# Letting a planner put five kinds of two-input operations on GpSimd instead of VectorE

## The chip, the cores and the metric

The kernel runs on one core of one Trainium2 chip. A core has five engines with queues of their own: TensorE (PE, matrix products), VectorE (DVE), ScalarE (ACT), GpSimd (POOL) and SyncE (SP, which here only issues transfers). Each works through its own instructions in the order in which they were written; semaphores between the engines make an instruction wait for what it needs. The metric is device microseconds of one execution, the median of the runs.

## The reference

A decoder block with two token mixers side by side, on 2048 tokens of 1024 channels, in float32:

```python
xn = rms_norm(x, g_pre);  proj = xn @ w_in      # r_x r_z m_x m_z m_o m_i m_f gate_r gate_m
u = causal_dwconv(r_x, rg_conv_w, rg_conv_b)    # 4 taps, then the RG-LRU
r, i = sigmoid(headwise(u, rg_w_a) + b_a), sigmoid(headwise(u, rg_w_x) + b_x)
a = exp(-8 * r * softplus(-lam));  b = sqrt(1 - a*a) * (i * u)
h_r = scan over tokens: h = a*h + b;            y_r = h_r * silu(r_z)
c = silu(causal_dwconv(m_x, ...)); q, k = headwise(c, ...); v = headwise(m_x, ...)
h_m = mlstm over chunks of 128 tokens, 4 heads of 256: gates, C and n states, running maximum
h_m = layer_norm(sigmoid(m_o) * h_m) * norm_g + skip * c;   y_m = h_m * silu(m_z)
y = sigmoid(gate_r) * (y_r @ w_branch_r) + sigmoid(gate_m) * (y_m @ w_branch_m)
out = x + rms_norm(y @ w_out, g_post)
```

## The kernel before, in words

**Tiling.** The 2048 tokens are four blocks of 512, taken two at a time (a "superblock"). Activations lie channels by tokens, 128 partitions by 512 tokens, 256 KB in a tile. Each operand of a float32 product is split into a rounded part and a rest (`split` and `wsplit`: the names end in h and l, or are `whi` and `wlo`), and a product is three matrix products (`mm3`). The rounding is a copy (a CAST in the profile, on ScalarE or VectorE), the rest a subtraction on VectorE.

**Stages.** In a superblock, `phase_a` makes the input projections with Strassen's seven products (`Pair`), runs the convolutions (`conv`, whose first three columns come from five small GpSimd operations into `hc`), the RG-LRU (`Rec`) and the gates, and stores the results in HBM. `phase_b` then takes eight heads one after another (four heads of two blocks, `Head`): `q` makes the queries, `s2` scales them with `eb` and splits them, `chunk` does the four chunks, `norm` and `back` finish the head; between them stand the products with `w_branch_r` and `w_branch_m` (`br`, `bm`) and with `w_out` (`out_half`, `out_last`), which keep TensorE fed while a head's chain runs.

**Who sets the order.** Nothing of this is emitted as it is written. `Plan` records every operation with its inputs, outputs and an estimated cost, and `order()` then runs a list schedule over the five engines: at each time an engine takes the operation with the smallest priority (its place in the program, moved by `early` and `urgent`) among those that are ready in the plan. The order it finds is what is emitted, engine by engine; on the chip each engine is bound to it. A result goes to another engine 150 ns later in the plan, and to TensorE another 400 ns later (`SYNC`, `SLACK`). An operation recorded with `either` has a second engine, which takes it when it has nothing of its own that is ready and the first engine is busy:

```python
elif item[2].seq <= limit and can(item[2]) and free[item[2].eng] > t + WORTH:
    pick = heapq.heappop(spare[e])
    op = pick[2]
    op.eng, op.cost, op.call = op.alt
```

The planner's costs in ns for n elements in a partition are, for GpSimd and for a VectorE operation with two wide inputs:

```python
if eng == "gpsimd":
    return 550 + n * 0.6, 0
...
    return 80 + 1.02 * n + (100 if len(ins) > 2 else 0), 0
```

that is 857 and 602 for 512 elements. In the kernel before, `either` serves only copies and squares, between ScalarE and VectorE (line 235 of the profile is an operation that went to its second engine, line 200 every other one). GpSimd has the small operations of `conv`, copies of states, the power -0.5 of the norms (`rstd`, `r`), a mask (`AFFINE_SELECT` on `mbc`), and issues most stores.

Of the kernel before, what the change touches and what calls it, by code (L numbers as in the profile page):

```python
# [12 lines left out]
ALU = mybir.AluOpType  # L13
# [376 lines left out]
def hybrid_kernel(ctx: ExitStack, tc: tile.TileContext, x, w_ch, w_mo, w_gate, w_q, w_k, w_v, w_out,  # L390
                  vec, gpost, bif, ident_d, triu_d, eye_d, xt_d, out):
    nc = Plan(tc.nc)
# [20 lines left out]
    def t2k(s="t", dt=F32):  # L413
        return nc.tile(tp, [P, 512], dt, "t", nm(s), ring=NSLOT - SPARE)

    def psum():
        return nc.tile(pp, [P, 512], F32, "ps", nm("ps"), ring=8)
# [19 lines left out]
    def vcol(v, j):  # L437
        return vecs[:, v, j:j + 1]
# [33 lines left out]
    def copy(out, in_):  # L472
        nc.either(("scalar", "copy", dict(out=out, in_=in_)), ("vector", "tensor_copy", dict(out=out, in_=in_)))


    def token_scale(b, keep=None):
        ss = small([P, NT, 2], "ss")
        ps = psum()
        for t in range(NT):
            r0 = b * T + t * P  # L480
            for q in range(2):
                xt = t2k("xh")
                with nc.urgent(0 if b else BPRI):
                    nc.sync.dma_start(out=xt, in_=x[r0:r0 + P, q * 512:(q + 1) * 512])
                if keep is None:
                    sq = xt
                else:
                    keep.append(xt)
                    sq = t2k("sq")
                acc = ss[:, t, q:q + 1]  # L490
                nc.either(("scalar", "activation", dict(out=sq, in_=xt, func=AF.Square, scale=1.0 / 32.0,
                                                        accum_out=acc)),
                          ("vector", "scalar_tensor_tensor", dict(out=sq, in0=xt, scalar=1.0 / D, in1=xt,
                                                                  op0=ALU.mult, op1=ALU.mult, accum_out=acc)))
            rstd = rms_scale(ss[:, t, :])
            dg = small([P, P], "dg")
            nc.vector.tensor_scalar(out=dg, in0=ident, scalar1=rstd, scalar2=None, op0=ALU.mult)
            with nc.urgent(BPRI):
                mmul(ps[:, t * P:(t + 1) * P], ones, dg, start=True, stop=True)
        rb = t2k("rb")  # L500
        with nc.urgent(BPRI):
            copy(rb, ps)
        return rb
# [290 lines left out]
    class Rec:  # L794
# [12 lines left out]
        def gate(self, bi, j, u, uhl):  # L807
            ghl = self.ghl
            th = []
            for q in range(2):  # L810
                pg = psum()
                o = (j % 2) * 256 + q * P
                mm3(pg, (ghl[0][:, o:o + P], ghl[1][:, o:o + P]), uhl, True, True)
                tt = t2k("tr")
                nc.scalar.activation(out=tt, in_=pg, func=AF.Sigmoid, bias=vcol(V_BX if q else V_BA, j))
                th.append(tt)
            nc.vector.tensor_tensor(out=u, in0=th[1], in1=u, op=ALU.mult)
            self.hold[bi, j] = (u, th[0])
            if len(self.hold) == 4:
                with nc.urgent(-LPRI):  # L820
                    self.scan()

        def scan(self):
            av = {}
            for (bi, j), (u, r) in self.hold.items():
                av[bi, j] = a = t2k("a")
                nc.scalar.activation(out=a, in_=r, func=AF.Exp, scale=nsp8[:, j:j + 1])
                nc.scalar.activation(out=r, in_=r, func=AF.Tanh, scale=sp8[:, j:j + 1])
                aq = t2k("aq")
                nc.scalar.activation(out=aq, in_=a, func=AF.Square)  # L830
                nc.vector.scalar_tensor_tensor(out=r, in0=aq, scalar=1.0, in1=r, op0=ALU.add, op1=ALU.mult)
            for u, r in self.hold.values():
                nc.scalar.activation(out=r, in_=r, func=AF.Sqrt, bias=tiny_t)
            for (bi, j), (u, r) in self.hold.items():
                nc.vector.tensor_tensor(out=u, in0=r, in1=u, op=ALU.mult)
                nc.vector.tensor_tensor_scan(out=r, data0=av[bi, j], data1=u, initial=hst.part(j)[:, j:j + 1],
                                             op0=ALU.mult, op1=ALU.add)
                nc.gpsimd.tensor_copy(out=hst.part(j)[:, j:j + 1], in_=r[:, 511:512])
                self.hr[bi, j] = r
# [143 lines left out]
    class Head:  # L983
# [91 lines left out]
        def s2(self):  # L1075
            h, cs, qs, G, eb = self.h, self.cs, self.qs, self.G, self.eb
            pS = psum()
            for c in range(NT):
                s = slice(c * P, (c + 1) * P)
                for k in range(2):  # L1080
                    mmul(pS[:, s], cs[k][:, s], qs[k][:, s], start=k == 0, stop=k == 1)
            wt = G.mbc[h]
            for c in range(NT):
                s = slice(c * P, (c + 1) * P)
                nc.scalar.activation(out=wt[:, s], in_=wt[:, s], func=AF.Exp, scale=-1.0, bias=G.A[:, c, h:h + 1])
            nc.vector.tensor_tensor(out=wt, in0=wt, in1=pS, op=ALU.mult)
            self.wt = split(wt, "wt")
            for k in range(2):
                nc.vector.tensor_tensor(out=qs[k], in0=qs[k], in1=eb, op=ALU.mult)
                qs[k] = split(qs[k], "q")  # L1090
            self.dn = small([P, NT], "dn")
            self.st = small([P, NT, 6], "st")
            self.mv = small([P, NT, 2], "mv")
# [59 lines left out]
        def back(self):  # L1153
            h, th, cs = self.h, self.th, self.cs
            for m in range(2):
                j = 2 * h + m
                pn = psum()
                for c in range(NT):
                    nc.tensor.transpose(pn[:, c * P:(c + 1) * P],
                                        th[c // 2][:, (c % 2) * DH + m * P:(c % 2) * DH + (m + 1) * P], ident)  # L1160
                nc.vector.scalar_tensor_tensor(out=cs[m], in0=pn, scalar=gh[:, j:j + 1], in1=cs[m],
                                               op0=ALU.mult, op1=ALU.add)
                tz = self.zz[m]
                nc.vector.tensor_tensor(out=tz, in0=cs[m], in1=tz, op=ALU.mult)
                nc.gpsimd.dma_start(out=self.Q["ym"][self.b % 2][j], in_=tz)


# [62 lines left out]
    def phase_b(sb, Q, fts, nxt):  # L1230
# [16 lines left out]
        def bm(bi, d, hooks=None):  # L1247
            tgd = branch(BM, d, [st["ym"]], [Q["gm"][bi][d]], {"hooks": hooks})[0]
            yp = t2k("ypl")
            with early():  # L1250
                nc.sync.dma_start(out=yp, in_=Q["yp"][bi][d])
            nc.vector.tensor_tensor(out=tgd, in0=tgd, in1=yp, op=ALU.add)
            st["y"].append(split(tgd, "y"))

        for u in range(8):
# [201 lines left out]
```

## Time and profile before

| | |
|---|---|
| median of 3 runs | 1977.0 us (1976.48 to 1977.06) |
| the profiled execution | 1975.61 us, span 1973.8 us |
| PE busy | 1955.6 us, 99% |
| DVE busy | 1600.5 us, 81% |
| ACT busy | 1158.6 us, 59% |
| POOL busy | 551.0 us, 28% |
| granted TensorE clock, mean | 0.998 |

The first superblock runs to about 1000 us, the second from there on. In each, the first half is `phase_a` (until about 560 us and 1530 us), the second `phase_b`. Busy PE time counts a matrix product from its start to its end, and the products overlap, so short delays between two of them do not show as idle time. In the rows a tile's number is left out, and digits at a name's end too.

### The profile page before, as it was taken

The page shows a single profiled execution, that of the slowest core. Times are in us where ns is not written, and L with a number is a line of the kernel's source. Part 1 is how long each engine was busy: PE and PEld are TensorE (multiplying, and loading weights), DVE is VectorE, ACT ScalarE, POOL GpSimd, SP SyncE. Part 2 cuts the span into 40 slices and gives each one's busy share as a digit, 9 for nine tenths or more (in the row PEclk, how much of TensorE's full clock was granted, in tenths as well). Part 3 has the DMA queues.
Part 4 walks back from the last instruction along what each step waited for, and adds up shares of the span by engine and source line. Part 5 has one row for each costly group of instructions (what it writes and reads, how often), then busy time and mean ns, then how long its engine had stood idle before and what let it go on. Part 6 is the DMA issues. An engine that isn't in the chain of part 4 may idle for free.

```text
span 1973.8 us, 30190 instructions
## 1 busy us (share of the span) xinstructions
PE 1955.6 (99%) x10240; PEld 1679.8 (85%) x10240; DVE 1600.5 (81%) x3052; ACT 1158.6 (59%) x2108; POOL 551.0 (28%) x864
## 2 busy tenths in 40 slices
PE   8999999999999999999999999999999999999998
PEld 8888888888898888887898888888888988888886
DVE  7997787978866889989579888788787677899783
ACT  6675665758555545654356768576585554465441
POOL 2544352443411111102037344434343111110010
PEclk9999999999999999999999999999999999999999
DMA  7224233232485557577372332413326843755661
GB/s 250 97 81 160 97 139 112 91 129 85 142 300 195 191 189 239 175 244 244 102 246 70 116 119 86 145 70 129 112 86 224 289 161 134 261 182 188 207 225 48
DMA packets 160987, 313.80 MB, mean 159 GB/s; under 512 B 19744, under 2 KB 40480, under 8 KB 160832
## 3 DMA queue, kind: packets, MB, share of 16 engines
q1 hardware_dynamic: 133440, 223.53, 34.1%
q0 software_dynamic: 27104, 88.21, 11.6%
q8 instruction: 80, 1.31, 0.3%
q14 instruction: 75, 0.61, 0.1%
q10 hardware_dynamic: 288, 0.13, 0.0%
HBM read 226.82 MB, written 84.97 MB: 158 GB/s over the span
## 4 chain that ended last, share of the span: by engine, by line
PE 96%; DVE 1%; POOL 1%; DMA 1%; issue 1%; ACT 0%; SPq 0%; POOLq 0%; ACTq 0%; DVEq 0%
PE ps L200 96%; POOL hc L200 1%; DVE wlo L200 0%; DMA xh<-in_x_dram 0%; DMA dth<-th 0%; DMA gp<-in_gpost_dram 0%; DVE o L200 0%; DVE u L200 0%; DMA dym<-mz 0%; DVE th L200 0%; POOL out_dram L200 0%; POOL rstd L200 0%; POOL r L200 0%; DVE a22l L200 0%; ACT uh L200 0%
## 5 line engine op out<-in xcount | busy, mean ns | idle before, releaser
L200 ACT CAST whi<-raw 128x512 fp32r<-128x512 f32 (+1 forms) x484 | 300.2, 621 | 469.7 <-PE ps L200 367.0
L200 DVE TENSOR_TENSOR wlo<-raw,whi 128x512 fp32r<-128x512 f32 (+1 forms) x576 | 394.6, 687 | 133.2 <-ACT whi L200 121.3
L200 DVE SCALAR_TENSOR_TENSOR u<-xq,vecs,u 128x511 f32<-128x511 f32 (+2 forms) x192 | 143.1, 745 | 8.5 <-ACT u L200 7.4
L200 DVE TENSOR_TENSOR raw<-raw,raw 128x512 f32<-128x512 f32 (+1 forms) x208 | 142.5, 687 | 1.7
L200 ACT ACT_TABLE_LOAD x89 | 114.2, 1283 | 5.9 <-DVE u L200 2.0
L200 POOL TENSOR_SCALAR h<-halo,vecs 128x2 f32<-128x2 f32 (+1 forms) x128 | 108.9, 864 | 1.3
L200 PE MATMUL ps<-ymh,wlo 128*128 128x512 f32 x256 | 100.2, 392 | 0.9 <-DVE wlo L200 0.9
L200 PE MATMUL ps<-yrh,whi 128*128 128x512 f32 x256 | 100.7, 394 | 0.0
L200 PE MATMUL ps<-yml,whi 128*128 128x512 f32 x256 | 100.5, 393 | 0.0
L200 PE MATMUL ps<-yrl,whi 128*128 128x512 f32 x256 | 100.4, 392 | 0.0
L200 PE MATMUL ps<-yrh,wlo 128*128 128x512 f32 x256 | 100.1, 391 | 0.0
L200 PE MATMUL ps<-ymh,whi 128*128 128x512 f32 x256 | 97.9, 394 | 0.5 <-ACT whi L200 0.5
L200 POOL TENSOR_SCALAR hc<-halo,vecs 128x3 f32<-128x3 f32 x64 | 81.6, 1275 | 8.1 <-DVE u L200 6.0
L200 POOL TENSOR_TENSOR rstd<-rsm,eps_t 128x1 f32<-128x1 f32 x32 | 20.2, 634 | 200.8 <-DVE rsm L200 186.1
L200 PE MATMUL ps<-a11h,whi 128*128 128x512 f32 x192 | 75.5, 393 | 0.0
L200 PE MATMUL ps<-whi,yh 128*128 128x512 f32 x192 | 75.5, 393 | 0.0
L200 PE MATMUL ps<-wlo,yh 128*128 128x512 f32 x192 | 75.1, 391 | 0.0
L200 PE MATMUL ps<-whi,yl 128*128 128x512 f32 x192 | 74.9, 391 | 0.0
L200 PE MATMUL ps<-a11l,whi 128*128 128x512 f32 x192 | 74.7, 389 | 0.0
L200 PE MATMUL ps<-a11h,wlo 128*128 128x512 f32 x192 | 74.7, 389 | 0.0
L200 PE MATMUL ps<-s3h,wlo 128*128 128x512 f32 x192 | 74.7, 389 | 0.0
L200 PE MATMUL ps<-s3h,whi 128*128 128x512 f32 x192 | 74.7, 389 | 0.0
(324 smaller groups left out, 6471.4 us busy)
## 6 DMA issues: line engine op xcount, KB each, us to landing
raw<-in_w_ch_dram SPq DMA_DIRECT2D x288, 256.0 KB, 2.8
raw<-in_w_out_dram SPq DMA_DIRECT2D x64, 256.0 KB, 2.9
raw<-in_w_mo_dram SPq DMA_DIRECT2D x48, 256.0 KB, 6.2
xh<-in_x_dram SPq DMA_DIRECT2D x32, 256.0 KB, 5.2
dth<-th POOLq DMA_DIRECT2D x32, 256.0 KB, 3.4
dgr<-tg POOLq DMA_DIRECT2D x32, 256.0 KB, 2.4
dyr<-tz POOLq DMA_DIRECT2D x32, 256.0 KB, 2.5
dmx<-xq POOLq DMA_DIRECT2D x32, 256.0 KB, 2.7
```

The lines of the kernel that those rows point to most:

```text
L200: getattr(eng.real, what)(*[real(v) for v in a], **{n: real(v) for n, v in kw.items()})
```

## The change

A helper `pair_op` records a two-input operation with VectorE first and GpSimd as the second engine, and five places use it: the product of the input gate and `u` (`gate`), the product with the square root (`scan`), the queries times `eb` (`s2`), the head's output times the silu gate (`back`), and the sum of the two branches (`bm`). There are 32 operations of each of the five, 160 in all, each 128x512 float32 with both inputs and the output in SBUF.

```diff
+    def pair_op(out, a, b, op):
+        k = dict(out=out, in0=a, in1=b, op=op)
+        nc.either(("vector", "tensor_tensor", k), ("gpsimd", "tensor_tensor", k))
...
-            nc.vector.tensor_tensor(out=u, in0=th[1], in1=u, op=ALU.mult)
+            pair_op(u, th[1], u, ALU.mult)
...
-                nc.vector.tensor_tensor(out=u, in0=r, in1=u, op=ALU.mult)
+                pair_op(u, r, u, ALU.mult)
...
-                nc.vector.tensor_tensor(out=qs[k], in0=qs[k], in1=eb, op=ALU.mult)
+                pair_op(qs[k], qs[k], eb, ALU.mult)
...
-                nc.vector.tensor_tensor(out=tz, in0=cs[m], in1=tz, op=ALU.mult)
+                pair_op(tz, cs[m], tz, ALU.mult)
...
-            nc.vector.tensor_tensor(out=tgd, in0=tgd, in1=yp, op=ALU.add)
+            pair_op(tgd, tgd, yp, ALU.add)
```

In the order that the planner makes of it, 103 of the 160 stand on GpSimd: 39 of the 64 `u<-tr,u`, 19 of the 32 `q<-q,eb`, 17 of the 32 `mz<-cs,mz` and 28 of the 32 `tgl<-tgl,ypl`. The order of the other operations changes with them on every engine, and six rounding copies go to VectorE that were on ScalarE.

The first place is the second head of the second superblock (`mz_16748` is the last product of the head before it, `q_17991` and `q_18034` are this head's queries, `wtl` and `ql` are rests that its first chunk needs). On VectorE before:

```order
L200 SCALAR_TENSOR_TENSOR cs_16738<-ps_18006,gh,cs_16738 128x512
L200 TENSOR_TENSOR mz_16748<-cs_16733,mz_16748 128x512
L200 TENSOR_TENSOR mz_16754<-cs_16738,mz_16754 128x512
L200 TENSOR_TENSOR wlo_18058<-raw_17578,whi_18024 128x512
L200 SCALAR_TENSOR_TENSOR kl_18065<-ps_18022,wg_17591,kh_18043 128x256
L200 SCALAR_TENSOR_TENSOR kl_18074<-ps_18031,wg_17591,kh_18047 128x256
L200 TENSOR_TENSOR mbc_17638<-mbc_17638,ps_18039 128x512
L200 TENSOR_TENSOR q_17991<-q_17991,eb_17726 128x512
L200 SCALAR_TENSOR_TENSOR kl_18065<-ps_18022,wg_17591,kh_18043 128x256
L200 SCALAR_TENSOR_TENSOR kl_18074<-ps_18031,wg_17591,kh_18047 128x256
L200 TENSOR_TENSOR q_18034<-q_18034,eb_17726 128x512
L200 TENSOR_TENSOR wtl_18102<-mbc_17638,wth_18090 128x512
```

Now, on VectorE, from the same place on:

```order
L200 TENSOR_TENSOR mz_16754<-cs_16738,mz_16754 128x512
L200 SCALAR_TENSOR_TENSOR kl_18062<-ps_18022,wg_17591,kh_18044 128x256
L200 SCALAR_TENSOR_TENSOR kl_18070<-ps_18031,wg_17591,kh_18049 128x256
L200 TENSOR_TENSOR mxl_18075<-mxr_17891,mxh_18013 128x512
L200 SCALAR_TENSOR_TENSOR kl_18062<-ps_18022,wg_17591,kh_18044 128x256
L200 SCALAR_TENSOR_TENSOR kl_18070<-ps_18031,wg_17591,kh_18049 128x256
L200 TENSOR_TENSOR mbc_17638<-mbc_17638,ps_18040 128x512
L200 TENSOR_TENSOR cl_18096<-cs_17909,ch_18065 128x512
L200 TENSOR_TENSOR ql_18103<-q_17991,qh_18094 128x512
L200 TENSOR_TENSOR wtl_18110<-mbc_17638,wth_18100 128x512
L200 TENSOR_TENSOR ql_18116<-q_18034,qh_18106 128x512
```

And on GpSimd:

```order
L200 TENSOR_TENSOR r_4139_17958<-r_4138_17944,eps_t 128x4
L235 TENSOR_TENSOR mz_16748<-cs_16733,mz_16748 128x512
L200 DMA dym_18052<-mz_16748 128x512
L200 DMA dym_18067<-mz_16754 128x512
L235 TENSOR_TENSOR q_17991<-q_17991,eb_17726 128x512
L235 TENSOR_TENSOR q_18034<-q_18034,eb_17726 128x512
```

One of the two `mz` products and both query products went over; they stand behind one another on GpSimd, with two store issues between, and VectorE does the rests `mxl` and `cl` where the products were.

The second place is on TensorE in `phase_a`, at the fourth gate product of a projection group (`uh` and `ul` are the parts of the convolved `u`, `gwh` and `gwl` those of its weights, `s1h` and `s1l` belong to the projection that runs meanwhile). Before:

```order
L200 MATMUL ps_5023<-s1h_620,whi_4956 128x512
L200 MATMUL ps_5023<-s1l_635,whi_4956 128x512
L200 MATMUL ps_5023<-s1h_620,wlo_4969 128x512
L200 MATMUL ps_5023<-s1h_665,whi_4956 128x512
L200 MATMUL ps_5023<-s1l_678,whi_4956 128x512
L200 MATMUL ps_5023<-s1h_665,wlo_4969 128x512
L200 MATMUL ps_5023<-s1h_707,whi_4956 128x512
L200 MATMUL ps_5023<-s1l_725,whi_4956 128x512
L200 MATMUL ps_5046<-uh_5030,gwh_4315 128x512
L200 MATMUL ps_5048<-uh_5030,gwh_4315 128x512
```

Now:

```order
L200 MATMUL ps_5026<-uh_5011,gwh_4315 128x512
L200 MATMUL ps_5030<-uh_5011,gwh_4315 128x512
L200 MATMUL ps_5034<-s1h_620,whi_4956 128x512
L200 MATMUL ps_5034<-s1l_635,whi_4956 128x512
L200 MATMUL ps_5026<-ul_5022,gwh_4315 128x512
L200 MATMUL ps_5026<-uh_5011,gwl_4332 128x512
```

The gate product has moved ahead of eight products of the projection; this is so in five of the eight projection groups, and with seven products in a sixth. On VectorE the first of the products with `u` that stood in front of this gate's rest `ul` (`u_4866<-tr_4985,u_4866`) has gone to GpSimd.

The third place is TensorE in the sixth head of the first superblock (`ymh`, `yml` belong to the branch product that fills the time, `wtl` and `qh` to the head's first chunk). Between the last product `q,cs` and the first that uses `qh` stood 24 products of 128x512 and 9 of 128x258; now there are 17 and 9. The rows ahead of the first use, before and then now:

```order
L200 MATMUL ps_9149<-ymh_7862,whi_9007 128x512
L200 MATMUL ps_9149<-yml_7946,whi_9007 128x512
L200 MATMUL ps_9149<-ymh_7862,wlo_9019 128x512
L200 MATMUL ps_9149<-ymh_7889,whi_9007 128x512
L200 MATMUL ps_9149<-yml_8224,whi_9007 128x512
L200 MATMUL ps_9131<-vh_8900,wtl_9145 128x258
L200 MATMUL ps_9131<-ch_8853,qh_9084 128x258
```

```order
L200 MATMUL ps_9089<-ymh_8236,whi_8949 128x512
L200 MATMUL ps_9089<-yml_8316,whi_8949 128x512
L200 MATMUL ps_9089<-ymh_8236,wlo_8963 128x512
L200 MATMUL ps_9089<-ymh_8245,whi_8949 128x512
L200 MATMUL ps_9089<-yml_8323,whi_8949 128x512
L200 MATMUL ps_9133<-vh_8920,wtl_9135 128x258
L200 MATMUL ps_9133<-ch_8848,qh_9131 128x258
```

The first chunk's product with the queries now comes before the branch product's second half is through, where it came after the next branch product had begun.

## The prediction

> **What bounds the kernel now.** I read the page's busy line and the shares of its chain of waits first, then what TensorE waited for, then the stages.
>
> ```profile
> PE 1955.6 (99%) x10240; PEld 1679.8 (85%) x10240; DVE 1600.5 (81%) x3052; ACT 1158.6 (59%) x2108; POOL 551.0 (28%) x864
> PE 96%; DVE 1%; POOL 1%; DMA 1%; issue 1%; ACT 0%; SPq 0%; POOLq 0%; ACTq 0%; DVEq 0%
> ```
>
> ```profile
> PE ps L200 <- DMA ident<-in_ident_dram: 3.9, 1, 3.9
> PE ps L200 <- ACT uh L200: 1.6, 2, 1.1
> PE ps L200 <- DMA xh<-in_x_dram: 1.1, 1, 1.1
> PE ps L200 <- DVE wlo L200: 0.9, 2, 0.5
> PE ps L200 <- ACT a11h L200: 0.8, 1, 0.8
> PE ps L200 <- ACT rb L200: 0.7, 1, 0.7
> PE ps L200 <- ACT whi L200: 0.5, 1, 0.5
> PE ps L200 <- DVE dg L200: 0.3, 1, 0.3
> ...
> 1965.59 0.02 issue
> ```
>
> TensorE is busy for 1955.6 of 1973.8 us and holds 96% of the chain. Of the 18.2 us that it idles, the waits make 9.8 and the end 8.2 (the last row is from the chain in order of time: the last product ends at 1965.59). `ident`, `xh`, `a11h`, `rb` and the longer `uh` wait belong to the first 81 us, before the first moved operation's result could matter. What is left for any change of VectorE's load to win are the other `uh` wait (1.6 - 1.1 = 0.5), `wlo` 0.9 and `whi` 0.5: **1.9 us, 0.1% of the time**. A view by stretches shows the same, and where VectorE is dense:
>
> ```profile
> 800.00:900.00 100.00, 99.62 (x583) 87.25 (x582) 92.68 (x214) 57.08 (x128) 10.54 (x18) 1.00 0.67 227
> 1300.00:1400.00 100.00, 100.00 (x443) 82.81 (x442) 84.48 (x140) 67.49 (x102) 44.77 (x70) 1.00 0.33 113
> 1700.00:1800.00 100.00, 100.00 (x583) 87.21 (x583) 92.53 (x206) 59.83 (x134) 12.48 (x25) 1.00 0.59 198
> ```
>
> Columns: stretch, length, busy PE, PE loads, DVE, ACT, POOL. VectorE reaches 93% in `phase_b`, but TensorE is full there too. So VectorE's 81% is no bound; the question is only whether the new order makes TensorE wait.
>
> **What a moved operation costs.** VectorE's price, from its groups kept apart by shape:
>
> ```profile
> L200 DVE TENSOR_TENSOR u<-tr,u 128x512 f32<-128x512 f32 x64 | 43.8, 684 | 3.5 <-ACT tr L200 3.5
> L200 DVE TENSOR_TENSOR q<-q,eb 128x512 f32<-128x512 f32 x32 | 23.2, 740 | 1.5 <-ACT eb L200 1.0 <-PE ps L200 0.6
> L200 DVE TENSOR_TENSOR tgl<-tgl,ypl 128x512 f32<-128x512 f32 x32 | 21.8, 683 | 0.0
> L200 DVE TENSOR_TENSOR mz<-cs,mz 128x512 f32<-128x512 f32 x32 | 21.1, 682 | 0.1
> ```
>
> About 0.68 us each; two in a row take 1.29 (first row below), so one more costs 0.60. The 103 that move free 103 x 0.60 = 62 us of VectorE. No two-input 128x512 operation runs on GpSimd in this trace. The nearest is the mask, with one input of this size:
>
> ```profile
> 877.28 1.29 DVE L200 TENSOR_TENSOR q<-q,eb 128x512 f32<-128x512 f32 x2
> 617.30 1.74 DVE L200 TENSOR_TENSOR q<-q,eb 128x512 f32<-128x512 f32 x2 [0.48 <-ACT eb L200]
> 617.34 1.16 POOL L200 TENSOR_SCALAR_AFFINE_SELECT mbc<-mbc 128x512 f32<-128x512 f32 x1 [5.04 <-ACT eb L200]
> 622.35 0.63 POOL L200 TENSOR_SCALAR_AFFINE_SELECT mbc<-mbc 128x512 f32<-128x512 f32 x1 [1.67 <-ACT eb L200]
> 621.92 0.68 DVE L200 TENSOR_TENSOR mbc<-mbc,ps 128x512 f32<-128x512 f32 x1
> 468.27 0.18 POOL L200 COPY halo<-xq 128x3 f32<-128x3 f32 x1
> ```
>
> Undisturbed it takes 0.63; a copy of three elements takes 0.18, so 512 elements cost 0.45. With a second input to fetch I take 0.18 + 2 x 0.45 = **1.1 us**, an estimate; bounds 0.63 (the second input is free) and 1.27 (two masks). The planner counts on 0.86.
>
> The same rows show a second price. At 617 us the mask began beside a pair of two-input products: the pair took 1.74 instead of 1.29, and the mask 1.16 instead of 0.63. They took turns: the mask waited for the first product (0.53), the second product for the mask (0.45). At 622 us a product with one input in PSUM, `mbc<-mbc,ps`, ran beside the mask at its usual 0.68. So a two-input operation on GpSimd holds up whatever VectorE wants to do with two SBUF inputs, for up to 1.1 us, and itself waits for up to 0.68. Per moved operation VectorE gains 0.60 and loses between 0 and 1.1: between -62 us and +51 us in all. VectorE is 81% busy and roughly three quarters of that has two SBUF inputs, which makes 0.6 x 1.1 = 0.66 lost: I expect VectorE's busy time **about unchanged, 1600 us**, and not 62 lower. POOL gains 103 x (1.1 + about 0.3 of waiting) = 144 us and stands at some 695.
>
> A rule of the Trainium skill speaks against the change: GPSIMD Engine Reference, section 4.1 (Engine selection), sends two-input elementwise work to VectorE, GpSimd being about half as fast; its section 3.1 has 4497 ns against 2293 for 2048 elements, by which a quarter is 1.12 us, an estimate. With 1.12 for 1.1 the sums here stay as they are; whether the slower engine costs time is the third rival below.
>
> **Where TensorE could wait: the heads.** The second head of the second superblock is the tight one of the kind whose two query products both move:
>
> ```profile
> 1614.73 1.40 DVE L200 SCALAR_TENSOR_TENSOR cs<-ps,gh,cs 128x512 f32<-128x512 f32 x2
> 1616.05 1.28 DVE L200 TENSOR_TENSOR mz<-cs,mz 128x512 f32<-128x512 f32 x2
> 1619.32 0.68 DVE L200 TENSOR_TENSOR q<-q,eb 128x512 f32<-128x512 f32 x1
> 1620.71 0.68 DVE L200 TENSOR_TENSOR q<-q,eb 128x512 f32<-128x512 f32 x1
> 1621.91 1.29 DVE L200 TENSOR_TENSOR ql<-q,qh 128x512 fp32r<-128x512 f32 x2
> 1617.03 1.16 POOL L200 DMA_DIRECT2D dym<-mz  x2 [5.03 <-DVE mz L200]
> 1623.70 0.28 PE L200 MATMUL ps<-ch,ql 128*128 128x258 f32 x1
> 1624.30 0.28 PE L200 MATMUL ps<-ch,ql 128*128 128x258 f32 x1
> ```
>
> Before, the second query product ends at 1621.39, the two rests `ql` at about 1622.6 and 1623.2, and TensorE takes them at 1623.70 and 1624.30: **1.1 us to spare**. Now: the first `mz` starts on GpSimd at 1615.6 (first `cs` done), ends at 1616.7; VectorE's `mz` is held until then and ends at 1617.4; the two store issues (1.16) end at 1618.0; the query products at 1619.1 and 1620.2, or up to 1.4 later with waits for VectorE. That is between 1.2 us earlier and 0.2 later than before: the detour over GpSimd is paid by VectorE's queue that it avoids. On VectorE there stand 5.2 us of work from there to the second `ql`, so 1617.4 + 5.2 = 1622.6, and up to 2.2 more where `mxl` and `cl` are held by the two query products: 1624.8 at worst, 0.5 late, and `wtl` perhaps 0.9. TensorE waits between 0 and 0.9 us there; I take 0.2, near the lower end, since half of the work between has a PSUM input. The order keeps TensorE's distance in this head; in the sixth and the last two heads of a superblock it shortens (in the sixth of the first by 7 products of 0.23, 1.6 us), which the planner does because it takes VectorE to be relieved; I give them the same bounds. Nine heads are tight like this (the second to fourth and sixth to eighth of the second superblock, the sixth to eighth of the first): 9 x 0.2 = **+1.8 us**, bounds 0 and 8.1.
>
> **The gates of phase_a.** The fourth gate product is now 8 products, 8 x 0.23 = 1.8 us, earlier:
>
> ```profile
> 473.12 0.68 DVE L200 TENSOR_TENSOR u<-tr,u 128x512 f32<-128x512 f32 x1
> 473.72 0.15 DVE L200 TENSOR_TENSOR u<-u,hc 128x3 f32<-128x3 f32 x1
> 475.18 0.61 ACT L200 CAST uh<-u 128x512 fp32r<-128x512 f32 x1
> 477.20 0.61 PE L200 MATMUL ps<-uh,gwh 128*128 128x512 f32 x2
> ```
>
> TensorE then wants `uh` at 477.20 - 1.81 = 475.4. `u` is done at 473.87, now 0.60 sooner as the product at 473.12 has gone, or 0.5 later if it holds VectorE for its whole 1.1 us; with the cast (0.61, and 0.1 between engines) `uh` is there between 474.0 and 475.1, in time. I take **0**; with one more hold it would be up to 0.7 late, in six groups 4.2. The products of `scan` feed only a store, which nobody reads before `phase_b`.
>
> **The rest.** On GpSimd the stores and the norm's power `r` now stand behind moved products, each up to 1.8 us later for one in front:
>
> ```profile
> POOL r L200 <- DVE r L200: 61.1, 14, 19.1
> POOL dym L200 <- DVE mz L200: 57.4, 13, 6.3
> ```
>
> GpSimd idled 61 us before 14 of the 16 `r` and 57 us before 13 of the 32 `dym` stores, so most find it free; no head's TensorE work waited for them before, and I price them at nothing, 1.8 us once at a superblock's end if not. The sums `tgl<-tgl,ypl` come every 5 us or slower, one product with `w_branch_m` apart; the last one's consumers are 21 products (4.8 us) behind it. For the 1.9 us of waits that a less crowded plan could remove I take **-0.5**. Sum: 1.8 + 0 - 0.5 = +1.3 us on the profiled execution's 1975.61, which is 1976.9; the median of the runs lies 1.4 above that execution, so **1978.3 us**, with a range of its own from 1975.1 (nothing lost, all 1.9 won) to 1982.7 (half of both upper bounds, 6.2, less 0.5).
>
> **The rivals.** First, slower: the holding decides. Each tight head loses its 0.9, since TensorE's order was made with 0.86 us and no holding in it, and every head starts from TensorE anew, so that the losses add: 9 x 0.9 = 8.1, **1985.1 us**. For it speak the shortened distances and the 93% of VectorE; against it that the moved products skip VectorE's queue. It decides from a loss of 0.6 us a head on (0.6 x 9 = 5.4). Second, faster: the waits at the superblock's ends go, -1.9, **1975.1 us**. The idle list allows no more, unless the end shrinks. Third, the rule named above taken as the bound: each of the 103 pays 1.1 - 0.60 = 0.5 us on the path, 51 us, **2028 us**. TensorE at 100% in two of the three stretches shown speaks against a path through VectorE. Fourth, the change does nothing of what it says: VectorE stays at 1600 us busy though 103 operations left it. That is part of my forecast and costs no time by itself.
>
> **How the numbers follow.** About no change 0.61, the heads 0.25, the waits removed 0.08, the rule as bound 0.02, a gain beyond the list of waits 0.04. A measurement of this kernel tells about 0.2% from no change, that is 4 us: 1973.0 to 1981.0. The forecast's upper part (0.05) and the first and third rival lie above, the second rival inside: faster 0.04, within 0.2% 0.64, slower 0.32. The range reaches from 1975 to 1987, past the middle of the first rival, which with the gates' 4.2 added would end at 1989.
>
> **What would show it.** Right: two-input POOL rows of 1.1 to 1.8 us; DVE busy within 30 us of 1600; PE waits on `qh`, `ql`, `wtl` of a few tenths in `phase_b`, none on `uh` after 100 us. The first rival: such waits of 0.6 and more in every tight head. Wrong altogether: DVE near 1540 (no holding), or PE idle in `phase_a`.

## The result, and the profile after

The changed kernel takes **2019.39 us** (median, 2018.09 to 2020.41) against 1977.03 (1976.48 to 1977.86) for the kernel before: a ratio of **1.0216, 95% interval 1.0203 to 1.0229**, 42 us slower. I had predicted 1978.3, with a range to 1987.

The page of the changed kernel, its busy line and the shares of its chain of waits:

```profile
PE 1975.1 (98%) x10240; PEld 1680.1 (83%) x10240; DVE 1624.4 (80%) x2955; ACT 1147.8 (57%) x2098; POOL 685.5 (34%) x967
PE 78%; DVE 12%; issue 5%; POOL 2%; DMA 2%; ACT 2%; SPq 0%; POOLq 0%; DVEq 0%; ACTq 0%
```

The span is 2018.4 us, 44.6 more. The busy times are as predicted: POOL 685.5 (I had 695), VectorE 1624.4 (I had 1600, within 30). But TensorE's share of the chain fell from 96% to 78%, and VectorE's rose from 1% to 12%. What TensorE now waits for (us in total, times, longest):

```profile
PE ps L200 <- DVE wlo L200: 5.7, 10, 2.4
PE ps L200 <- ACT yh L200: 4.6, 1, 4.6
PE ps L200 <- DVE th L200: 4.1, 7, 0.9
...
PE ps L200 <- DVE cl L200: 2.4, 2, 1.2
PE ps L200 <- ACT wth L200: 2.2, 3, 0.9
PE ps L200 <- DVE wtl L200: 2.1, 4, 0.6
```

Only the waits that leave TensorE idle stand there. Products are pipelined, so I also summed how much later than usual for its shape each product starts after the one before (differences over 30 ns, the usual being the median, without the first 12 us): 21.5 us before, 64.6 after. The 43 more, by what the late product reads: weights in `phase_a` 13, operands of a head's chunks (`wth`, `wtl`, `cl`, `qh`, `ql`) 11, the transposes of `th` 8, the last products (`woh`, `yh`) 5, products at half clock 4, the rest 2.

The products on GpSimd and, below them, three kinds of VectorE work with two SBUF inputs that did not move (groups kept apart by shape; busy time, then mean ns):

```profile
L235 POOL TENSOR_TENSOR u<-tr,u 128x512 f32<-128x512 f32 x39 | 56.7, 1457 | 71.9 <-ACT tr L200 71.9
L235 POOL TENSOR_TENSOR tgl<-tgl,ypl 128x512 f32<-128x512 f32 x28 | 48.5, 1734 | 116.7 <-DVE tgl L200 110.6 <-DMA raw<-in_w_out_dram 4.3 <-DMA mxr<-dmx 1.8
L235 POOL TENSOR_TENSOR q<-q,eb 128x512 f32<-128x512 f32 x19 | 24.4, 1305 | 4.7 <-ACT xh L200 2.3 <-PE ps L200 2.3
L235 POOL TENSOR_TENSOR mz<-cs,mz 128x512 f32<-128x512 f32 x17 | 23.2, 1365 | 77.5 <-DVE cs L200 77.4
```

```profile
L200 DVE TENSOR_TENSOR wlo<-raw,whi 128x512 fp32r<-128x512 f32 x560 | 405.8, 726 | 129.4 <-ACT whi L200 120.2 <-DMA tgl<-dgr 2.2 <-DVE whi L235 0.5
L200 DVE TENSOR_TENSOR mxl<-mxr,mxh 128x512 fp32r<-128x512 f32 x32 | 29.2, 912 | 2.0 <-ACT mxh L200 2.0
L200 DVE TENSOR_TENSOR cl<-cs,ch 128x512 fp32r<-128x512 f32 x32 | 27.2, 851 | 0.0
```

A product takes about 1.3 us when nothing stops it, 1.48 on the mean of all 103. `wlo` was at 686 ns on the mean before, `mxl` at 677, `cl` at 682. Three places in order of time show how that reaches TensorE. First, `phase_a` (start, length, what ran):

```profile
254.64 4.33 DVE L200 TENSOR_TENSOR wlo<-raw,whi 128x512 fp32r<-128x512 f32 x1
254.67 3.74 POOL L235 TENSOR_TENSOR u<-tr,u 128x512 f32<-128x512 f32 x3
...
259.02 0.51 PE L200 MATMUL ps<-s1h,wlo 128*128 128x512 f32 x1 [2.44 <-DVE wlo L200]
```

One VectorE operation of 0.69 us takes 4.33: it stands through **three** products in a row on GpSimd, and TensorE wants its result. This is the worst of the ten `wlo` waits; the other nine are 0.4 us on the mean. Second, two places in the heads:

```profile
657.11 3.27 DVE L200 TENSOR_TENSOR mxl<-mxr,mxh 128x512 fp32r<-128x512 f32 x1
657.26 2.56 POOL L235 TENSOR_TENSOR q<-q,eb 128x512 f32<-128x512 f32 x2
...
662.56 0.36 PE L200 MATMUL ps<-vh,wth 128*128 128x258 f32 x1 [0.89 <-ACT wth L200]
```

```profile
1797.54 1.67 POOL L235 TENSOR_TENSOR tgl<-tgl,ypl 128x512 f32<-128x512 f32 x1 [3.89 <-DVE tgl L200]
1797.98 1.26 DVE L200 TENSOR_SCALAR r<-r 128x4 f32<-128x4 f32 x1
...
1799.32 1.42 POOL L200 TENSOR_TENSOR r<-r,eps_t 128x4 f32<-128x4 f32 x1
...
1802.88 0.30 PE L200 MATMUL ps<-ident,th 128*128 128x128 f32 x1 [1.83 <-issue]
```

At 657 us a rest that nobody needs yet, `mxl`, is held by both query products; behind it on VectorE's queue stands `mbc<-mbc,ps`, from which `wth` is made. At 1798 us a step of the norm on four columns, held by a sum, ends 1.26 us after its start (0.17 where nothing holds it); the power `r` comes after it, two rests stand ahead of `th` on VectorE's queue, and the transposes of `th` wait 1.83. Third, the end:

```profile
1958.94 1.88 DVE L200 TENSOR_TENSOR wol<-raw,woh 128x512 fp32r<-128x512 f32 x3
...
1959.10 2.87 POOL L235 TENSOR_TENSOR tgl<-tgl,ypl 128x512 f32<-128x512 f32 x1 [4.24 <-DVE tgl L200]
...
1962.65 0.69 DVE L200 TENSOR_TENSOR yl<-tgl,yh 128x512 fp32r<-128x512 f32 x1 [1.83 <-ACT yh L200]
...
1963.26 2.49 DVE L200 TENSOR_TENSOR wol<-raw,woh 128x512 fp32r<-128x512 f32 x4
...
1965.66 0.68 DVE L200 SCALAR_TENSOR_TENSOR tgl<-tgl,ps 128x512 f32<-128x512 f32 x1
...
1966.43 1.64 POOL L235 TENSOR_TENSOR tgl<-tgl,ypl 128x512 f32<-128x512 f32 x1 [4.46 <-DVE tgl L200]
...
1968.77 0.79 PE L200 MATMUL ps<-woh,yh 128*128 128x512 f32 x1 [4.56 <-ACT yh L200]
```

Here GpSimd is the one that stands: its second last sum (2.87) waits through VectorE's row of three `wol`. `yl` on VectorE's queue then waits 1.83 for `yh`, made from that sum, with the next `wol` and the step of the last `tgl` behind it; the last sum starts late, and TensorE idles 4.56 us. With each of the two long waits the granted clock falls to half for a while (columns: stretch, length, busy PE, PE loads, DVE, ACT, POOL, granted clock, DMA share, GB/s):

```profile
260.00:265.00 5.00, 5.00 (x16) 3.93 (x16) 5.00 (x7) 2.21 (x4) 2.70 (x4) 0.66 0.15 52
...
1970.00:1975.00 5.00, 5.00 (x15) 3.92 (x15) 0.69 (x1) 0.69 (x2) 0.00 (x0) 0.63 0.00 0
```

### The profile page after: what moved, and what is told of

The parts are those of the page before. It is cut to its first block, busy times and chain, and to the rows that moved or that the text cites. A ratio compares the mean times of both kernels' runs of the same rounds, so it can differ in the third digit from the quotient of the medians.

```text
span 2018.4 us, 30291 instructions
## 1 busy us (share of the span) xinstructions
PE 1975.1 (98%) x10240; PEld 1680.1 (83%) x10240; DVE 1624.4 (80%) x2955; ACT 1147.8 (57%) x2098; POOL 685.5 (34%) x967
## 3 DMA queue, kind: packets, MB, share of 16 engines
q8 instruction: 80, 1.31, 0.3%
## 4 chain that ended last, share of the span: by engine, by line
PE 78%; DVE 12%; issue 5%; POOL 2%; DMA 2%; ACT 2%; SPq 0%; POOLq 0%; DVEq 0%; ACTq 0%
PE ps L200 78%; DVE wlo L200 3%; DVE u L200 1%; POOL hc L200 1%; DVE raw L200 1%; DVE tr L200 1%; POOL tgl L235 1%; DVE cl L200 0%; DVE kl L200 0%; DVE th L200 0%; DVE tz L200 0%; DMA raw<-in_w_out_dram 0%; DVE z L200 0%; DVE yl L200 0%; DVE tgl L200 0%
## 5 line engine op out<-in xcount | busy, mean ns | idle before, releaser
L200 DVE TENSOR_TENSOR wlo<-raw,whi 128x512 fp32r<-128x512 f32 (+1 forms) x576 | 417.0, 726 | 138.6 <-ACT whi L200 129.3
L200 DVE SCALAR_TENSOR_TENSOR u<-xq,vecs,u 128x511 f32<-128x511 f32 (+2 forms) x192 | 148.3, 772 | 8.8 <-ACT u L200 7.6
L200 DVE TENSOR_TENSOR raw<-raw,raw 128x512 f32<-128x512 f32 (+1 forms) x208 | 150.9, 727 | 2.7 <-DMA raw<-in_w_mo_dram 0.6
L200 POOL TENSOR_SCALAR h<-halo,vecs 128x2 f32<-128x2 f32 (+1 forms) x128 | 102.3, 808 | 1.4
L235 POOL TENSOR_TENSOR tgl<-tgl,ypl 128x512 f32<-128x512 f32 x28 | 48.5, 1734 | 116.7 <-DVE tgl L200 110.6
L235 POOL TENSOR_TENSOR u<-tr,u 128x512 f32<-128x512 f32 x39 | 56.7, 1457 | 71.9 <-ACT tr L200 71.9
L200 PE MATMUL ps<-s2h,wlo 128*128 128x512 f32 x192 | 77.3, 403 | 1.1 <-DVE wlo L200 0.8
L200 PE MATMUL ps<-s1h,wlo 128*128 128x512 f32 x192 | 75.9, 395 | 2.4 <-DVE wlo L200 2.4
L200 PE MATMUL ps<-a12h,wlo 128*128 128x512 f32 x192 | 75.5, 393 | 0.0
L200 PE MATMUL ps<-s2h,whi 128*128 128x512 f32 x192 | 75.3, 392 | 0.0
```

Of the source, the lines that this page charges most:

```text
L200: getattr(eng.real, what)(*[real(v) for v in a], **{n: real(v) for n, v in kw.items()})
L235: getattr(real, what)(**{n: v.real() if isinstance(v, View) else v for n, v in k.items()})
```

## The experiments

Four things change at once when a product moves: the planner writes another order; the product is late by its length on GpSimd; VectorE is held; and VectorE is relieved. My theory after the result: **the holding of VectorE, which the planner doesn't know of, costs the 42 us.** Rivals: the order as such; the price, which the planner takes for 0.86 us; and the plain length of the product on TensorE's path. All runs compare with the kernel before, which took 1977.3 to 1977.9 us beside them.

**The order, with the products back on VectorE.** The plan believes in GpSimd; what is issued runs on VectorE:

```diff
-                        op.eng, op.cost, op.call = op.alt
+                        if op.alt[0] == "gpsimd":
+                            op.eng, op.cost = op.alt[:2]
+                        else:
+                            op.eng, op.cost, op.call = op.alt
```

> The changed kernel's plan, kept as it is, but the 103 products that the planner gave to GpSimd are issued on VectorE, at the place in time that the plan gave them. No two-input 128x512 operation runs on GpSimd; VectorE has 62 us more to do than the plan thinks. Holding theory (a GpSimd product keeps VectorE from its SBUF inputs, and TensorE's order was made without that): the holds are gone, 1977 to 1985 us. Lateness theory (GpSimd's results come after 1.3 us and more where the plan has 0.86, VectorE has time to spare): VectorE's results are not late either, 1977 to 1985. Order theory (the new order of the other operations is worse, whichever engine does the products): 2010 to 2020.

Measured: 1996.15 us, 1.0095 (1.0080 to 1.0110). None of the three forecasts: 18.5 us stay although GpSimd holds nothing. The next run tells whether that is the order.

**The order, with products of almost no length.**

```diff
+            cut = (lambda v: v[:, 0:3]) if eng == "gpsimd" else (lambda v: v)
-            getattr(real, what)(**{n: v.real() if isinstance(v, View) else v for n, v in k.items()})
+            getattr(real, what)(**{n: cut(v).real() if isinstance(v, View) else v for n, v in k.items()})
```

> The changed kernel in its own order, but the 103 products on GpSimd work on 3 of their 512 columns (the other 509 of each are left out): all places, waits and queues stay, and only the 1.29 us of each and what it holds are gone. Theory (the products' length and the holding of VectorE cost the 43 us, and the run with the plan kept but the products on VectorE lost its 18 us because VectorE then has 62 us more than the plan gave it): 1974 to 1980 us, the plan as it was meant. Rival (the order itself, with stores and powers of the norm behind products on GpSimd, loses those 18 us): 1990 to 1998 us.

Measured: **1977.05 us**, 0.9994 (0.9984 to 1.0003). The busy line of this run's page:

```profile
PE 1955.9 (99%) x10240; PEld 1680.2 (85%) x10240; DVE 1552.0 (79%) x2955; ACT 1153.3 (58%) x2098; POOL 570.4 (29%) x967
```

The same instructions at the same places cost nothing once the products are short, so the order alone is not the cause. And VectorE relieved (1552.0 instead of 1600.5) wins nothing that can be measured. The run before it is now readable: it has this order, but VectorE has the 103 products back (1607.4 busy in its page, 55 more than here). The plan had given that time away, and taking it back costs 18.5 us, though VectorE's total is what it was before the change.

**The price told to the planner.** 1290 ns for a product on GpSimd, instead of 857; 102 move.

```diff
+        if eng == "gpsimd" and what == "tensor_tensor" and n == 512:
+            return 1290, 0
```

> The changed kernel, with the planner's cost of a GpSimd product of 512 elements at 1290 ns, its undisturbed time in the trace, in place of 857. It still moves 102. Lateness theory: the order now allows for it, 1977 to 1985 us. Holding theory: the plan still knows nothing of VectorE being held, 2005 to 2020. Order theory: another order of the same kind, 2005 to 2020.

Measured: 2012.31 us, 1.0176 (1.0161 to 1.0192). An order made with the right price gets 7 of the 42 us back.

**The hold told to the planner.** On top of the price, the plan doesn't let a product on GpSimd and a VectorE operation with two wide inputs in SBUF (or a copy from SBUF) run at one time; 104 move.

```diff
+        wide = [v for v in views if v.buf.tag != "ps" and v.shape[-1] > 4]
+        op.port = eng.name == "vector" and (len(wide) > 1 or what == "tensor_copy" and len(wide) == 1)
...
+                if op.port or (op.alt and e == op.alt[0]):
+                    other = {"vector": "gpsimd", "gpsimd": "vector"}.get(e)
+                    if other and (e == "vector" and op.port or e == "gpsimd"):
+                        cost += max(0.0, held[other] - t)
+                        held[e] = t + cost
                 op.at = t
```

> As the run before it, and the plan also lets a GpSimd product and a VectorE operation with SBUF inputs only exclude each other: each waits in the plan for the other's end. It moves 104 products. Holding theory: TensorE's order now allows for the holds, 1976 to 1988 us. Lateness theory: no better than with the price alone. Order theory: 2005 to 2020.

Measured: **1983.01 us**, 1.0028 (1.0017 to 1.0039). Its page and the largest of its groups of products:

```profile
PE 1958.1 (99%) x10240; PEld 1678.9 (85%) x10240; DVE 1614.5 (81%) x2951; ACT 1154.1 (58%) x2105; POOL 683.8 (35%) x968
```

```profile
L239 POOL TENSOR_TENSOR u<-tr,u 128x512 f32<-128x512 f32 x51 | 77.5, 1525 | 91.7 <-ACT tr L202 91.7
```

The products are no shorter (1.49 us on the mean), GpSimd is as busy as in the changed kernel (POOL 683.8 for 685.5) and VectorE nearly so (1614.5 for 1624.4), and there are as many pairs and triples of products without a gap (12 each, counted in the traces). VectorE is held as often: 92 of its operations take over 0.15 us longer than the kernel before's median for the same tile and shape, 76 us in all, against 90 and 82 in the changed kernel. Yet 36 of the 42 us are gone. So it is not the amount of holding that costs, but **holding that the order was not made for**. Only the longest holds are missing too: none is over 1.4 us here, where the changed kernel has four (3.6, 2.6, 2.6 and 1.6 us, 10 us together).

What costs this plan its 5 us was asked by giving it products of three columns, the same edit as above:

> The run whose planner was told the hold (1983.0 us), its order unchanged, with its 104 products on 3 of 512 columns (the rest left out). If the 5 us that it lost are what holding leaves, 1976 to 1979 us; if its order costs them, 1981 to 1984 us.

Measured: 1974.94 us, 0.9989 (0.9980 to 0.9998). Its order costs nothing, and the 8 us between the two runs are what the products' length and holding still do. It also shows how little there was to win: with VectorE relieved at no price at all, 0.1%.

**Late, but holding nothing.** In the kernel before, a power on four columns takes 1.04 us on GpSimd and VectorE runs on beside it. So each product of three columns got such a power behind it:

```diff
+            if eng == "gpsimd":
+                part = k["out"][:, 0:4].real()
+                real.tensor_tensor(out=part, in0=part, in1=self.pw.real(), op=ALU.pow)
```

In the changed kernel's order:

> The changed kernel in its own order; each of the 103 products on GpSimd works on 3 of its 512 columns and a power of 4 columns, made in place, follows it (the other columns are left out, and the 4 are other numbers). In the kernel before, such a power takes 1.04 us on GpSimd, and the VectorE operations beside it take 2 ns more than usual, so GpSimd is as late as in the changed kernel and holds nothing. Theory (what costs is that VectorE is held): 1977 to 1984 us. Rival (the products' own length is on TensorE's path): 2005 to 2020 us.

Measured: 1992.63 us, 1.0081 (1.0066 to 1.0096), between the two forecasts. What its VectorE waits for longest on GpSimd (us in total, times, longest), and the busy line of its page:

```profile
DVE tr L200 <- POOL u L239: 12.4, 12, 1.5
```

```profile
PE 1962.6 (98%) x10240; PEld 1678.3 (84%) x10240; DVE 1552.0 (78%) x2955; ACT 1147.7 (58%) x2098; POOL 692.5 (35%) x1070
```

VectorE is held by nothing (1552.0, as with three columns), but it waits 12.4 us for a late `u` at the head of its queue: the plan counted on 0.86, and product and power take 1.59 together (1.48 in the changed kernel). So a part of the 42 us can be had by lateness alone. The same pair of edits in the order whose planner knew the price separates the two cleanly:

> The run whose planner was told the price of 1.29 us (2012.3 us), its order unchanged, with each of its 102 products on 3 columns and the power of 4 columns behind it (the rest of the columns is left out): about as long on GpSimd as the product, planned for, and nothing held. Theory (with the price planned for, what is left is the holding alone): 1977 to 1986 us, so that the holding costs 26 to 35 us there. Rival (being late on GpSimd costs it even when the planner knows the price): 1990 us or more.

Measured: **1978.77 us**, 1.0009 (0.9999 to 1.0019).

```profile
PE 1958.4 (99%) x10240; PEld 1679.7 (85%) x10240; DVE 1555.7 (79%) x2972; ACT 1146.9 (58%) x2086; POOL 703.7 (36%) x1068
```

GpSimd is as long at it as with the products (1.62 us each for 1.52; POOL 703.7 for 688.1) in the same order, and only the holding is missing: VectorE is 70 us less busy (1555.7 for 1625.7), and **33.5 us** are gone (2012.31 - 1978.77). This is the run on which the verdict rests. VectorE waits for a late `u` here too, 9.9 us in nine times, and the kernel loses 1.5 us; so the 12.4 us of that wait in the run before do not measure what lateness cost there.

**Holding, but not late.** The attempt at the reverse: behind each product of three columns four of 95 columns, into a tile that nobody reads.

```diff
+            for _ in range(4 if eng == "gpsimd" else 0):
+                src = k["in1"][:, 0:95].real()
+                real.tensor_tensor(out=self.scr.real(), in0=src, in1=k["in0"][:, 0:95].real(), op=ALU.mult)
```

> The changed kernel in its own order; each of the 103 products works on 3 of its 512 columns, and then four products of 95 columns follow on GpSimd, into a tile that nobody reads (the product's other columns are left out). Together about as long as the product; GpSimd's next instructions wait for them, the product's reader doesn't. Theory (holding): VectorE's busy time rises from the 1552 us of the run with three columns to 1600 or more, and the time to 2000 to 2018 us. Rival (the product's own lateness): VectorE's busy time rises as much, the time stays at 1977 to 1988 us.

Measured: 2023.55 us, 1.0236 (1.0219 to 1.0253). The time is just above the theory's, and the reason is another, by the same two views:

```profile
DVE tr L200 <- POOL pad L239: 25.3, 27, 1.9
```

```profile
PE 1973.3 (98%) x10240; PEld 1680.3 (83%) x10240; DVE 1576.1 (78%) x2955; ACT 1149.2 (57%) x2098; POOL 804.0 (40%) x1379
```

VectorE is held for 24 us only (1576.1 - 1552.0). The small products took turns with VectorE, so that the four take 2.35 us together, and VectorE waits 25.3 us to write `tr` anew, which they still read. It shows that GpSimd's lateness costs much when it is long, and nothing of the holding: inconclusive.

**Extra products in the old order.** The kernel before, with 103 products beside the real ones, which stay on VectorE; they are written to a tile that nobody reads, and are planned at no cost. For this tile the weight tiles had to shrink from 576 to 528 columns, and no weight is wider than that.

```diff
-SW = 576
+SW = 528
...
+        nc.vector.tensor_tensor(out=out, in0=a, in1=b, op=op)
+        if out.buf.name + "|" + (b if a.buf is out.buf else a).buf.name in PLACES:
+            nc.free = True
+            nc.gpsimd.tensor_tensor(out=scr, in0=out, in1=out, op=ALU.mult)
+            nc.free = False
```

> The kernel before and its order, all five kinds on VectorE; at each of the 103 places a GpSimd product of the result with itself is added, into a scratch tile that nobody reads, planned at no cost so that the other engines' orders stay as before (but for a few neighbours exchanged). Holding theory: VectorE is held as in the change and has not lost its own 103 products, so 2005 to 2035 us. Lateness theory: nobody waits for the added results, 1977 to 1980. Order theory: the order is that of before, 1977 to 1980.

Measured: 2016.00 us, 1.0197 (1.0180 to 1.0214), as the holding theory said, but its trace showed something else too: a 512-column product of TensorE came every 231 ns on the median, instead of 227, everywhere but at the end. So the narrower tiles were run alone:

> The kernel before with one edit: the weight tiles are 528 columns wide instead of 576, as in the run with the extra products, and there is no product on GpSimd. In that run the median start-to-start distance of TensorE's 512-column products was 231 ns, against 227 in the kernel before, in every 100 us of the span, also where GpSimd had next to no products. If the width (where the tiles lie) does that, this run has it too: 6719 x 4 ns = 27 us at most, 1996 to 2004 us, and only 12 to 20 of the 38 us of the run with the extra products belong to GpSimd. If the extra products do it, this run takes 1976 to 1979 us.

Measured: 1997.77 us, 1.0099 (1.0082 to 1.0116), with VectorE and GpSimd untouched:

```profile
PE 1977.9 (99%) x10240; PEld 1679.2 (84%) x10240; DVE 1603.9 (80%) x3052; ACT 1162.2 (58%) x2108; POOL 539.8 (27%) x864
```

20 of the 38 us were the control's own. What is left for the extra products is 18.2 us (2016.0 - 1997.8), less than the theory had (28 at least) and far more than the rivals (3 at most). There VectorE's busy time rises by 47 us (1651.0 in the page for 1603.9), nobody waits for the products, and the order was made for a VectorE with its full load. The added products also read one tile as both inputs and are shorter, 1.03 us at the least and 1.36 on the mean, so the run holds VectorE less than the change does.

**One part alone.** Only `u` may move (39 do), then only the others (64 do); the other calls of `pair_op` are VectorE operations again.

> One part alone: only the two products of phase_a (u) may go to GpSimd; 39 do. By the stalls counted in the changed kernel's trace, the weights of phase_a (+13 us), the wait for th (+8), the gates (+1) and half of the slow clock (+2) belong to them: 1997 to 2004 us if the parts add up. If the loss needs several kinds of products together, under 1987 us.

> The other part alone: only the query products (q), mz and the sums tgl may go to GpSimd; 64 do. By the stalls counted in the changed kernel's trace, those before the chunk products (+11 us), the end (+5) and half of the slow clock (+2) belong to them: 1992 to 1998 us if the parts add up, so that this run's and the gates' losses together make the 42 us. If the loss needs several kinds together, under 1985 us.

Measured: 1994.52 us, 1.0083 (1.0068 to 1.0098), and 2005.28 us, 1.0137 (1.0122 to 1.0152). Each lies outside its own forecast, the first below and the second above, but the losses, 16.6 and 27.4, make 44.0 for the 42: the parts add up, so no meeting of several kinds is needed. TensorE's waits in the run with `u` alone, then with the others alone:

```profile
PE ps L200 <- DVE wlo L200: 6.3, 11, 2.5
```

```profile
PE ps L200 <- ACT yh L200: 4.6, 1, 4.6
...
PE ps L200 <- DVE th L200: 3.5, 6, 0.9
PE ps L200 <- DVE cl L200: 2.4, 2, 1.2
PE ps L200 <- DVE wtl L200: 2.4, 5, 0.6
```

My split was off in one point: the waits for `th` belong to the second part (by the starts of TensorE's products between 7 and 8 us there, nothing in the first), not to `u`.

| run | GpSimd's products | VectorE busy, us | time, us |
|---|---|---|---|
| before | none | 1600.5 | 1977.0 |
| changed kernel | 1.48 us, hold | 1624.4 | 2019.4 |
| its order, on VectorE | none | 1607.4 | 1996.2 |
| its order, late without holding | 1.59 us, no hold | 1552.0 | 1992.6 |
| its order, three columns | short | 1552.0 | 1977.1 |
| price told | 1.52 us, hold | 1625.7 | 2012.3 |
| price told, late without holding | 1.62 us, no hold | 1555.7 | 1978.8 |
| hold told | 1.49 us, hold | 1614.5 | 1983.0 |
| hold told, three columns | short | 1546.4 | 1974.9 |

## Why the prediction was wrong

**What bounds the kernel: right.** TensorE does, and 1.9 us was all that a relief of VectorE could win. With the products cut to three columns, the changed kernel's order came out 0.8 us below the kernel before, which is no difference, and the order that knew the hold 2.5 us below (0.4 to 4.0 by its interval).

**What a moved operation costs: half right.** The price of 1.1 us was too low: 1.28 to 1.31 undisturbed, just above my upper bound of 1.27, and 1.48 on the mean with waits, where I had 1.4. The holding per product was well sized: VectorE got 72 us back (1624.4 - 1552.0), 0.70 for each of the 103, where I took 0.66, and the relief was 55 us (1607.4 - 1552.0) instead of 62. But the bound of 1.1 us for one hold was wrong: I read the pair at 617 us as taking turns, and in a row of products without a gap VectorE does not always get its turn. Of nine such rows in the changed kernel that held a VectorE operation at the border of two products, it got in between them in four and was passed over in five (the longest took 3.27 and 4.33 us).

**The step that failed** is the one from there to TensorE: VectorE's busy time "about unchanged, 1600 us", therefore nothing to price outside nine tight heads. A busy time that is unchanged in total is not unchanged for the order. The planner had taken VectorE to be relieved and had placed the rests `wlo` and `wtl`, the steps of `th` and everything else of VectorE's queue with 55 us less in between; giving just that back, with no holding, costs 18.5 us. I saw this once, for the three heads of a superblock whose distance shortens ("which the planner does because it takes VectorE to be relieved"), and gave them the bounds of the other heads instead of carrying it to every place where TensorE reads what VectorE makes.

So the terms of the sum, one by one:
- *Heads, +1.8, at most 8.1.* The place was right and the size was not: the operands of the chunks are 11 us later, with a start that is 1.05 and 0.75 us late within one head (at 662.56 and 663.62 us), since `mxl` in front of `wth` was held by both query products.
- *Gates of phase_a, 0, at most 4.2.* `uh` is indeed nearly in time (TensorE waits 2.1 us for it in all, 1.6 before). What is late is the work behind the held operations on VectorE's queue, `wlo`, which I had not looked at; `u` alone costs 16.6 us.
- *Norm and stores, nothing.* The idle time of 61 us before 14 powers was an average over the span. TensorE loses 8 us at the transposes of `th`, at four heads' ends. At two of them (809 and 1799 us, more than half of it) a sum on GpSimd stands just ahead of `r`, as in the rows at 1798 us; at the other two (848 and 1840 us) no moved product is near, and why VectorE is late there was not followed.
- *Last sums, nothing, "21 products (4.8 us) behind it".* The cover was used up by the last two sums, 2.87 and 1.64 us, and by `yl` waiting at the head of VectorE's queue: 4.56 us, and half a clock with it. That the sums come "every 5 us or slower" was misread besides: in the kernel before two start at 1904.99 and 1905.60.
- *Waits removed, -0.5.* With three columns 0.8 in this order, which can't be told from nothing; the second rival's 1975.1 was reached only by another order, the one that knew the hold, and with products of almost no length (1974.9).

**The rivals.** The first, that the holding decides, had the mechanism, but only at nine places, and so 8 us; the holding cost 33.5 where it could be taken away alone. The third came nearest in time (2028 for 2019) by luck: it had each of the 103 pay for its length on the path. Length without holding costs 15 us where the planner is wrong about it, and 1.5, hardly to be told from nothing, where it knows it. The rule of the Trainium skill beside it (GPSIMD Engine Reference, section 4.1, Engine selection) is borne out in its advice. The estimate by section 3.1 of that page, a quarter of 4497 ns or 1.12 us, lies below the 1.28 to 1.31 of this trace. The fourth, VectorE still at 1600 though relieved, came true, and I took it to cost no time.

What stays open: how the 18.5 us (VectorE relieved in the plan only), the 15 (lateness) and the holding share the 42 in the changed kernel's own order. They don't add, since a VectorE that is held has less time to wait for a late product; only in the order with the price told are they taken apart.

## What to carry to other kernels

When a planner moves work to another engine, ask first what the order will be made of: relief that the chip doesn't give is spent by the plan all the same, at every place where the bounding engine reads what the relieved one makes. An engine's busy time that comes out unchanged is then a warning, not a comfort; price the queue of work behind each held or late instruction, not the consumers of the moved operation alone. And where two engines share something, put that into the planner's cost model before the second engine: price and hold together took the loss from 42 to 5 us here, and still left nothing to win, since TensorE was the bound.

## What the runs showed of the hardware

**Who has the shared access can keep it over several instructions.** The Trainium skill (SBUF — State Buffer, "Who interferes with whom") says that a VectorE instruction with two SBUF inputs contends with a GpSimd instruction that reads SBUF, that the lock is exclusive, and that the order of issue decides who blocks. The rows of two-input products above agree with the exclusion. The order of issue doesn't describe all of them: `wlo` at 254.64 began 0.03 us ahead of the first of three products and stood until the third was done, and the sum at 1959.10 stood through VectorE's row of `wol` for 2.87 us. In other rows the engines took turns:

```profile
1941.85 3.00 POOL L235 TENSOR_TENSOR tgl<-tgl,ypl 128x512 f32<-128x512 f32 x2 [3.04 <-DVE tgl L200]
1942.29 1.40 DVE L200 TENSOR_TENSOR wlo<-raw,whi 128x512 fp32r<-128x512 f32 x1
```

This `wlo` got in between the two sums, and the second sum took 1.74 us. In the changed kernel the five VectorE operations that were passed over began 0.03 to 0.15 us ahead of a product's start, the four that got their turn 0.13 to 0.44 us behind one. An operation with one input and four columns was held too (`r<-r`, 1.26 us).

**Not all of GpSimd's work holds VectorE.** A power on four columns takes 1.04 us there when nothing stops it, and 103 of them left VectorE's total unchanged (1552.0 with and without them).

**TensorE's half clock came with waits of 2.44 us and less.** The Trainium skill (TensorE: Matmul & The Clock Gate, "What's actually happening") has it after an idle window of some 3.4 us. Here one wait of 2.44 us was enough for a stretch of 3.41 us at half speed (260.25 to 263.66 in the clock's record of the changed kernel), and the wait of 4.56 us went with one of 6.83 that began within it (1966.91). In the run without `u` on GpSimd two waits of 0.73 and 0.92 us, the second ending at 842.75, were followed by 3.41 us at half speed from 842.93 on; the wait of 1.83 us in the changed kernel was followed by none.

**The width of the weight tiles can cost 1%.** With 528 instead of 576 columns for each weight tile, the 6719 products of 512 columns start 231 ns apart on the median, for 227, and the kernel takes 20 us more. The edit moves these tiles and those behind them in SBUF; whether the place of a tile does it, and which, was not asked.
